# FFN blocks: units of the second product set between the Strassen pairs of the next quarter

## The chip, the cores and the metric

The kernel runs on one core of a Trainium2 chip. The time is the device time of one execution in microseconds (us); of several runs the median is taken.

## The reference

A forward pass over 512 positions of width 1024 in float32: four layers with different mixers, each followed by an FFN, and a fifth block with its own mixers and an FFN. Every FFN is the same computation, and it is the part that this change touches:

```python
def _sqrelu_mlp(h, w1, w2):
    return jnp.square(jax.nn.relu(h @ w1)) @ w2

x = x + _sqrelu_mlp(_rmsnorm(x, norm_mlp_g[i]), mlp_w1[i], mlp_w2[i])
```

Here x is 512 x 1024, w1 is 1024 x 4096 and w2 is 4096 x 1024. The mixers are a gated linear recurrence (twice), a gated spatial unit, a short convolution and, in the last block, a long one with several branches (layer M below), cross attention and an FFN.

## The kernel before

**Stages.** The program emits twelve stages one behind the other: A0 F0 B F1 C F2 A1 F3 M X G N2. F0 to F3 and G are the five FFN blocks, A0, B, C and A1 the mixers between them, M and X the mixers of the last block, N2 the last norm. Activations stand transposed, so a tile of 128 x 512 holds 128 of the 1024 (or 4096) features for all 512 positions.

**Products.** A float32 product is made from three matmuls in fp32r: each operand is split into a high half (a cast) and a low half (what is left), and `mm3` (L896 to L898) adds high x high, high x low and low x high in psum. Weights are split on the chip: ScalarE casts the high half (whi), VectorE subtracts it from the raw tile for the low half (wlo).

**Units.** The usual piece of work is a unit: weights of 8 x 128 x 128 (a raw tile of 128 x 1024 that holds eight 128 x 128 blocks), 24 matmuls of 512 columns, one psum tile. Its cast is L839, its low half L840. Two raw tiles (NRAW) and three pairs of weight tiles (NW) go round; weights are prepared two tiles ahead of the product that is being issued (PREP).

**FFN quarters.** An FFN block (`ffn`, L993) goes through w1's 4096 columns in four quarters. The first product of quarter 0 is eight plain units on the unscaled x with the norm's factor applied behind (relu, square and split make u, eight tiles per quarter, as uhi and ulo). The first product of quarters 1 to 3 is four Strassen pairs each: `pair` (L1058) makes two tiles of u from two column blocks of w1 with seven products of half the positions in place of eight, 84 matmuls of 256 columns. Four of the seven products use sums of weight blocks that `_mixed` (L780) makes on VectorE (ws, L796 and L798), each product's weights (128 x 512) are cast by L825 and subtracted by L807, and two consecutive products share one weight tile. The low half is put off: `_low` (L803) issues it together with the next product's cast. What the products give is combined on VectorE into two tiles: tu, the odd one (cm at L1074 and L1075, tu at L1078), and cy, the even one (L1080 and L1083). Each of the two then goes through three ScalarE instructions (relu L940, square L1005, cast L1006) and one VectorE subtraction (ulo, L1009). These are put off too, in the list `todo`: tu's to the pair's products 5 and 6, cy's to the next pair's products 0 and 1; in a quarter's last pair cy's are issued at once.

Behind a quarter's first product, `project` (L973) runs the eight units of the second product, which add their result to x (L979). A unit needs all eight u of its quarter; the two u that come last are asked for last (`ks`). So the order of work in a block is: eight units of w1, eight units of w2, then three times four pairs and eight units of w2.

**What stands beside.** During quarter 0 a side thread (`background`) normalizes x and prepares the operands for the Strassen products, 32 steps: two at each unit of w1 but the first, one at each third step of the units of w2, the rest behind them.

**Extra products.** The first four products of each run of pairs (EXTRA) are prepared ahead of the three weight tiles, in eight slots (whx, wlx) of the common store for activation tiles, which has 75 slots of 128 x 512 (NSLOT).

**Order.** The pairs and units run in the order of the code. In stages with several threads, such as M, a planner (`schedule`, L413) picks the next step by a model of the engines' clocks; that clock runs on from the program's first stage to the last, and the picks depend on where it stands.

The lines that fix which weights are ready when:

```python
    def _low(self):
        if self.late is not None:
            low, w, high = self.late
            self.nc.vector.tensor_sub(low, w, rt(high))
            self.late = None
...
        while self.pos + len(self.ready) < n and self.tids[self.pos + len(self.ready)] <= self.base[self.pos] + PREP:
            while self.loaded < n and self._load():
                pass
            self._prep()
```

Of the kernel before, what the change touches and what calls it, by code (L numbers as in the profile page):

```python
# [13 lines left out]
ALU = mybir.AluOpType  # L14
# [3 lines left out]
P = 128  # L18
# [12 lines left out]
NRAW = 2  # L31
NW = 3
PREP = 2
EXTRA = 4
NSLOT = 75
LAST = 0
TOL = 300
# [161 lines left out]
def rt(t):  # L199
    return t.bitcast(F32)  # L200
# [451 lines left out]
class Net:  # L652
    def __init__(self, tc, nc, es, d, plan=None):
# [4 lines left out]
        else:  # L658
# [4 lines left out]
            for unit in self.order:  # L663
                two = isinstance(unit[0], str)
                run = run + 1 if two else 0
                extra = two and run <= EXTRA
                t += not (extra or two and half)
# [325 lines left out]
    def ffn(self, inp, nxt, w1, w2):  # L993


        nc = self.nc
        hn, op, todo = [], {}, []

        def relu2(t, k, when):


            def rounded():
                u[k] = self.t("uhi", S, F32R), self.t("ulo", S, F32R)
                self.act(t, t, AF.Relu)
                nc.scalar.square(t, t)  # L1005
                nc.scalar.copy(u[k][0], t)  # L1006

            def rest():
                nc.vector.tensor_sub(u[k][1], t, rt(u[k][0]))  # L1009

            return [(when[0], rounded), (when[1], rest)]

        def square(t):
            hi, lo = self.t("uhi", S, F32R), self.t("ulo", S, F32R)
            nc.scalar.square(t, t)
            nc.scalar.copy(hi, t)
            nc.vector.tensor_sub(lo, t, rt(hi))
            return hi, lo

        def normed():  # L1020
            r = inp.scale()
            for m in range(NCH):
                t = self.t("hn")
                nc.vector.scalar_tensor_tensor(t, inp.xs[m], self.v(inp.gname, inp.g0 + m), r, ALU.mult, ALU.mult)
                hn.append(t)
                yield

        def background():
            yield from normed()
            yield from operands()  # L1030

        def operands():

            a, b = HALF
            for c in range(4):
                p, q = hn[c], hn[c + 4]
                s, t = self.t("ts"), self.t("ts")
                nc.vector.tensor_sub(s[:, a], p[:, b], p[:, a])
                nc.vector.tensor_sub(s[:, b], q[:, b], s[:, a])
                yield  # L1040
                nc.vector.tensor_sub(t[:, a], q[:, b], p[:, b])
                nc.vector.tensor_sub(t[:, b], q[:, a], s[:, b])
                yield
                if c % 2 == 0:
                    raw = self.t("thi", S, F32R), self.t("tlo", S, F32R)
                h = HALF[c % 2]
                nc.scalar.copy(raw[0][:, h], p[:, a])
                nc.vector.tensor_sub(raw[1][:, h], p[:, a], rt(raw[0][:, h]))
                op[0, c] = [x[:, h] for x in raw]
                yield  # L1050
                for src, i, j in ((q, 1, 2), (s, 4, 5), (t, 6, 3)):
                    w = self.t("thi", S, F32R), self.t("tlo", S, F32R)
                    nc.scalar.copy(w[0], src)
                    nc.vector.tensor_sub(w[1], src, rt(w[0]))
                    op[i, c], op[j, c] = [x[:, a] for x in w], [x[:, b] for x in w]
                    yield

        def pair(s0, s1, j, last):  # L1058

            a, b = HALF  # L1060
            ps, add = {}, nc.vector.tensor_add
            for i, (k, bank, h) in enumerate(PRODUCTS):
                w = self.w_pair(s0, s1, i)
                for f in [f for n, f in todo if n == i]:
                    f()
                if h == 0:
                    ps[bank] = self.psum()
                for c in range(4):
                    self.mm3(ps[bank][:, HALF[h]], w[0][:, c], w[1][:, c], *op[k, c], c == 0, c == 3, 357)
                if i == 1:  # L1070
                    y, m = self.t("cy"), self.t("cm")
                    nc.scalar.copy(y[:, a], ps[0][:, a])
                elif i == 2:
                    add(m[:, a], y[:, a], ps[0][:, b])  # L1074
                    add(m[:, b], m[:, a], ps[1][:, a])  # L1075
                elif i == 4:
                    t = self.t("tu")
                    add(t.rearrange("p (c n) -> p c n", c=2), m[:, None, b].to_broadcast([P, 2, 256]),  # L1078
                        ps[2].rearrange("p (c n) -> p c n", c=2))
                    add(y[:, b], m[:, a], ps[2][:, b])  # L1080
                    todo[:] = relu2(t, j + 1, (5, 6))
                elif i == 6:
                    add(y, y, ps[3])  # L1083
                    todo[:] = relu2(y, j, (0, 1))
                    if last:
                        while todo:
                            todo.pop(0)[1]()
                self.lock(i < 6)
                yield

        for q in range(4):
            u = []
            if q == 0:
                side = background()
                for j in range(8):
                    ps = yield from self.mm(w1[j], inp.h)
                    r = inp.scale()
                    t = self.t("tu")
                    nc.vector.scalar_tensor_tensor(t, ps, 0.0, r, ALU.max, ALU.mult)
                    u.append(square(t))  # L1100
                    if j:
                        next(side, None)
                        next(side, None)
                    yield
                product = self.project(w2[q], u, None)
                for n, need in enumerate(product):
                    if n % 3 == 0:
                        next(side, None)
                    yield need
                for _ in side:  # L1110
                    pass
                hn.clear()
                continue
            u = [None] * 8
            for j in range(0, 8, 2):
                yield from pair(w1[q * 8 + j], w1[q * 8 + j + 1], j, j == 6)
            yield from self.project(w2[q], u, nxt if q == 3 else None, ks=(0, 1, 2, 3, 4, 5, 7, 6))


    def lru_consts(self):  # L1120
# [1052 lines left out]
```

## Time and profile before

| | before |
|---|---|
| three runs, us | 3529.70, 3520.67, 3526.14 (median 3526.14) |
| profiled execution, us | 3520.22 |
| its span, us | 3518.4 |
| mean granted clock of TensorE | 0.993 |
| TensorE busy (matmuls), us | 3404.5 |
| TensorE weight loads, us | 2783.7 |
| VectorE busy, us | 2313.7 |
| ScalarE busy, us | 1531.6 |
| GpSimd busy, us | 524.5 |
| DMA | 334.91 MB, 95 GB/s on the mean |

The span goes from the first to the last instruction of the profiled execution; its own time lies 1.8 us above it. In the profile PE is TensorE's matmuls, PEld its weight loads, DVE is VectorE, ACT is ScalarE, POOL is GpSimd, SP issues the loads. L840 is line 840 of the kernel. An instruction is named by what it writes and reads (wlo<-raw,whi), its count by x. A matmul's busy time runs from its start to its modelled end, so that a matmul which is held up in the middle counts as busy for longer.

### The profile page before, as it was taken

To read this page: it belongs to the slowest core of one execution; us is meant where nothing else is said; L and a number is where in the kernel's file an instruction comes from. 1 tells how busy PE (TensorE), PEld (TensorE's weight loads), DVE (VectorE), ACT (ScalarE), POOL (GpSimd) and SP (SyncE) were. 2 spreads that over 40 slices of the span, in tenths; PEclk is the share of its full clock that TensorE was granted. 3 is DMA by queue.
4 is the path that set the end of the run, shared out by engine and by line. 5 is a ranking of instruction groups with operands and counts; after the bars stand their busy time and mean duration, and the time that the engine had idled before them with its cause. 6 is when DMAs were issued, how large, how long until landed. Compare 5 with 4: busy or idle time off the path is not lost. (4 is left out here: it accounts for less than half of the span.)

```text
span 3518.4 us, 48137 instructions
## 1 busy us (share of the span) xinstructions
PE 3404.5 (97%) x18850; PEld 2783.7 (79%) x18850; DVE 2313.7 (66%) x3618; ACT 1531.6 (44%) x2393; POOL 524.5 (15%) x845
## 2 busy tenths in 40 slices
PE   8999999999999999999999999999999999999998
PEld 6778888888887888887877888777767787778887
DVE  7677666567666567666767666776568566567665
ACT  5634444344443234444554444443354344334444
POOL 1020002110001010001011000546245400110002
PEclk9999999999999999999999999999999999999999
DMA  3223222222223323222223222332223344223221
GB/s 118 86 84 114 96 96 84 84 90 90 96 96 103 96 90 102 96 96 85 86 83 119 84 91 87 108 95 84 73 82 125 91 131 154 63 80 115 96 96 61
DMA packets 127237, 334.91 MB, mean 95 GB/s; under 512 B 18592, under 2 KB 21792, under 8 KB 127008
## 3 DMA queue, kind: packets, MB, share of 16 engines
q1 hardware_dynamic: 119712, 322.37, 29.1%
q0 software_dynamic: 7296, 9.46, 1.1%
q8 instruction: 148, 2.42, 0.3%
q14 instruction: 81, 0.66, 0.1%
HBM read 317.07 MB, written 14.68 MB: 94 GB/s over the span
## 5 line engine op out<-in xcount | busy, mean ns | idle before, releaser
L840 DVE TENSOR_TENSOR wlo<-raw,whi 128x1024 fp32r<-128x1024 f32 (+3 forms) x466 | 609.6, 1308 | 178.3 <-ACT whi L839 168.5
L839 ACT CAST whi<-raw 128x1024 fp32r<-128x1024 f32 (+3 forms) x466 | 463.6, 999 | 492.6 <-PE ps L897 370.1
L896 PE MATMUL ps<-hhi,whi 128*128 128x512 f32 x1512 | 619.8, 410 | 11.6 <-ACT whi L839 6.1
L898 PE MATMUL ps<-hhi,wlo 128*128 128x512 f32 x1512 | 600.8, 397 | 7.4 <-DVE wlo L840 7.4
L897 PE MATMUL ps<-hlo,whi 128*128 128x512 f32 x1512 | 601.2, 398 | 5.8 <-DVE hlo L476 5.8
L896 PE MATMUL ps<-uhi,whi 128*128 128x512 f32 (+1 forms) x1296 | 508.6, 392 | 10.4 <-ACT uhi L1006 10.4
L897 PE MATMUL ps<-ulo,whi 128*128 128x512 f32 (+1 forms) x1296 | 508.3, 392 | 3.4 <-DVE ulo L1009 3.4
L898 PE MATMUL ps<-uhi,wlo 128*128 128x512 f32 (+1 forms) x1296 | 507.1, 391 | 0.0
L898 PE MATMUL ps<-thi,wlo 128*128 128x256 f32 x1440 | 415.1, 288 | 24.2 <-DVE wlo L807 20.6
L896 PE MATMUL ps<-thi,whi 128*128 128x256 f32 x1440 | 407.5, 283 | 7.0 <-ACT whi L825 6.7
L897 PE MATMUL ps<-tlo,whi 128*128 128x256 f32 x1440 | 404.1, 281 | 0.0
L896 PEld LDWEIGHTS ps<-hhi,whi 128*128 128x128 f32 x1512 | 286.0, 189 | 86.7 <-ACT hhi L475 6.9
L898 PEld LDWEIGHTS ps<-hhi,wlo 128*128 128x128 f32 x1512 | 285.7, 189 | 76.1 <-DVE wlo L840 9.1
L897 PEld LDWEIGHTS ps<-hlo,whi 128*128 128x128 f32 x1512 | 285.6, 189 | 72.3 <-DVE hlo L476 10.6
L898 PEld LDWEIGHTS ps<-thi,wlo 128*128 128x128 f32 x1440 | 270.9, 188 | 45.7 <-DVE wlo L807 45.7
L896 PEld LDWEIGHTS ps<-uhi,whi 128*128 128x128 f32 x1296 | 243.3, 188 | 71.2 <-ACT uhi L1006 16.8
L897 PEld LDWEIGHTS ps<-ulo,whi 128*128 128x128 f32 x1296 | 243.3, 188 | 62.8 <-DVE ulo L1009 8.1
L898 PEld LDWEIGHTS ps<-uhi,wlo 128*128 128x128 f32 x1296 | 243.3, 188 | 55.3
L896 PEld LDWEIGHTS ps<-thi,whi 128*128 128x128 f32 x1440 | 271.1, 188 | 13.1 <-ACT whi L825 13.1
L979 DVE TENSOR_TENSOR x<-x,ps 128x512 f32<-128x512 f32 x176 | 120.5, 685 | 230.2 <-PE ps L898 230.2
L897 PEld LDWEIGHTS ps<-tlo,whi 128*128 128x128 f32 x1440 | 271.2, 188 | 0.0
L896 PE MATMUL ps<-hi,whi 128*128 128x512 f32 x616 | 247.6, 402 | 9.0 <-ACT hi L945 5.2
(371 smaller groups left out, 5363.5 us busy)
## 6 DMA issues: line engine op xcount, KB each, us to landing
raw<-in_mlp_dram SPq DMA_DIRECT2D x160, 512.0 KB, 3.7
raw<-in_mlp_dram SPq DMA_DIRECT2D x192, 256.0 KB, 5.1
raw<-in_u_ffn_w_dram SPq DMA_DIRECT2D x40, 512.0 KB, 3.7
raw<-in_a_win_dram SPq DMA_DIRECT2D x39, 512.0 KB, 3.6
raw<-in_w_rest_dram SPq DMA_DIRECT2D x34, 512.0 KB, 3.7
raw<-in_w_rkv_dram SPq DMA_DIRECT2D x26, 512.0 KB, 3.7
raw<-in_c_win_dram SPq DMA_DIRECT2D x24, 512.0 KB, 3.7
raw<-in_u_ffn_w_dram SPq DMA_DIRECT2D x48, 256.0 KB, 5.2
```

The lines of the kernel that those rows point to most:

```text
L839: nc.scalar.copy(h[:, c], r[:, c])
L840: nc.vector.tensor_sub(l[:, c], r[:, c], rt(h[:, c]))
L896: nc.tensor.matmul(ps, wh, xh, start=start, stop=False)
L897: nc.tensor.matmul(ps, wh, xl, start=False, stop=False)
L898: nc.tensor.matmul(ps, wl, xh, start=False, stop=stop)
L979: self.nc.vector.tensor_add(self.x[m], self.x[m], ps)
```

## The change

Behind the eight units of quarter 0's first product, the units of a quarter's second product no longer run as eight in a row behind four pairs in a row. A string gives the order for each quarter q of 0 to 2: U is a unit of the second product of quarter q, P a pair of quarter q + 1's first product. For quarter 0 it is UUUUUUPUUPPP, for quarters 1 and 2 UUUUPUUPUUPP. The eight units of quarter 3 come last, as before. Per block five pairs (of twelve) then stand alone between units, four stand in twos and three in a three. The list `todo` is worked off at a pair's products as before, or at every odd step of a unit. The side thread advances at every even step of a unit of quarter 0. EXTRA is 0, so all products of pairs are prepared in the three weight tiles. Two quarters of u (eight tiles each, uhi and ulo) are alive at the same time.

```diff
@@ -31,7 +31,7 @@
 NRAW = 2
 NW = 3
 PREP = 2
-EXTRA = 4
+EXTRA = 0
 NSLOT = 75
 LAST = 0
 TOL = 300
@@ -996,7 +996,7 @@
         nc = self.nc
         hn, op, todo = [], {}, []
 
-        def relu2(t, k, when):
+        def relu2(t, u, k, when):
 
 
             def rounded():
@@ -1055,14 +1055,14 @@
                     op[i, c], op[j, c] = [x[:, a] for x in w], [x[:, b] for x in w]
                     yield
 
-        def pair(s0, s1, j, last):
+        def pair(s0, s1, u, j, last):
 
             a, b = HALF
             ps, add = {}, nc.vector.tensor_add
             for i, (k, bank, h) in enumerate(PRODUCTS):
                 w = self.w_pair(s0, s1, i)
-                for f in [f for n, f in todo if n == i]:
-                    f()
+                while todo and todo[0][0] <= i:
+                    todo.pop(0)[1]()
                 if h == 0:
                     ps[bank] = self.psum()
                 for c in range(4):
@@ -1078,43 +1078,49 @@
                     add(t.rearrange("p (c n) -> p c n", c=2), m[:, None, b].to_broadcast([P, 2, 256]),
                         ps[2].rearrange("p (c n) -> p c n", c=2))
                     add(y[:, b], m[:, a], ps[2][:, b])
-                    todo[:] = relu2(t, j + 1, (5, 6))
+                    todo.extend(relu2(t, u, j + 1, (5, 6)))
                 elif i == 6:
                     add(y, y, ps[3])
-                    todo[:] = relu2(y, j, (0, 1))
+                    todo.extend(relu2(y, u, j, (0, 1)))
                     if last:
                         while todo:
                             todo.pop(0)[1]()
                 self.lock(i < 6)
                 yield
 
-        for q in range(4):
-            u = []
-            if q == 0:
-                side = background()
-                for j in range(8):
-                    ps = yield from self.mm(w1[j], inp.h)
-                    r = inp.scale()
-                    t = self.t("tu")
-                    nc.vector.scalar_tensor_tensor(t, ps, 0.0, r, ALU.max, ALU.mult)
-                    u.append(square(t))
-                    if j:
-                        next(side, None)
-                        next(side, None)
-                    yield
-                product = self.project(w2[q], u, None)
-                for n, need in enumerate(product):
-                    if n % 3 == 0:
+        def unit(q, m):
+            ps = yield from self.mm(w2[q][m], us[q], ks=late if q else None)
+            nc.vector.tensor_add(self.x[m], self.x[m], ps)
+            yield
+
+        us, late = [[None] * 8 for _ in range(4)], (0, 1, 2, 3, 4, 5, 7, 6)
+        side = background()
+        for j in range(8):
+            ps = yield from self.mm(w1[j], inp.h)
+            r = inp.scale()
+            t = self.t("tu")
+            nc.vector.scalar_tensor_tensor(t, ps, 0.0, r, ALU.max, ALU.mult)
+            us[0][j] = square(t)
+            if j:
+                next(side, None)
+                next(side, None)
+            yield
+        for q in range(3):
+            u, j, m = us[q + 1], 0, 0
+            for step in "UUUUUUPUUPPP" if q == 0 else "UUUUPUUPUUPP":
+                if step == "P":
+                    yield from pair(w1[q * 8 + 8 + j], w1[q * 8 + 9 + j], u, j, j == 6)
+                    j += 2
+                    continue
+                for n, need in enumerate(unit(q, m)):
+                    if n % 2 == 1 and todo:
+                        todo.pop(0)[1]()
+                    if q == 0 and n % 2 == 0:
                         next(side, None)
                     yield need
-                for _ in side:
-                    pass
-                hn.clear()
-                continue
-            u = [None] * 8
-            for j in range(0, 8, 2):
-                yield from pair(w1[q * 8 + j], w1[q * 8 + j + 1], j, j == 6)
-            yield from self.project(w2[q], u, nxt if q == 3 else None, ks=(0, 1, 2, 3, 4, 5, 7, 6))
+                m += 1
+            us[q] = None
+        yield from self.project(w2[3], us[3], nxt, ks=late)
 
 
     def lru_consts(self):
```

Every engine executes the same instructions as before (16415 rows on TensorE in both), but for two table loads fewer on ScalarE in layer M; what changes is their order. Three places show it.

VectorE before, from the end of a quarter's third pair (ulo of tu, the last sum of y) into its fourth (mixed weights ws, low halves wlo, ulo of y, the sums cm and tu):

```order
L807 TENSOR_TENSOR wlo<-raw,whi 128x512
L1009 TENSOR_TENSOR ulo<-tu,uhi 128x512
L1083 TENSOR_TENSOR cy<-cy,ps 128x512
L807 TENSOR_TENSOR wlo<-ws,whi 128x512
L798 TENSOR_TENSOR ws<-raw,ws 128x512
L807 TENSOR_TENSOR wlo<-raw,whi 128x512
L1009 TENSOR_TENSOR ulo<-cy,uhi 128x512
L1074 TENSOR_TENSOR cm<-cy,ps 128x256
L1075 TENSOR_TENSOR cm<-cm,ps 128x256
L807 TENSOR_TENSOR wlo<-ws,whi 128x512
L840 TENSOR_TENSOR wlo<-raw,whi 128x1024
L1078 TENSOR_TENSOR tu<-cm,ps 128x512
```

VectorE at the end of a pair that stands alone, changed: the same sums tu and cy and the same ulo, but with the low halves of the two units that follow (L840) among them, and the ws of the next pair behind.

```order
L807 TENSOR_TENSOR wlo<-ws,whi 128x512
L840 TENSOR_TENSOR wlo<-raw,whi 128x1024
L1078 TENSOR_TENSOR tu<-cm,ps 128x512
L1080 TENSOR_TENSOR cy<-cm,ps 128x256
L840 TENSOR_TENSOR wlo<-raw,whi 128x1024
L1009 TENSOR_TENSOR ulo<-tu,uhi 128x512
L1083 TENSOR_TENSOR cy<-cy,ps 128x512
L796 TENSOR_TENSOR ws<-raw 128x512
L798 TENSOR_TENSOR ws<-ws,raw 128x512
L807 TENSOR_TENSOR wlo<-raw,whi 128x512
L798 TENSOR_TENSOR ws<-raw 128x512
L1009 TENSOR_TENSOR ulo<-cy,uhi 128x512
```

So the low half of one unit stands ahead of the sum for tu and that of a second ahead of ulo at the end of a single pair too, where at the third pair's end before only weights of the next pair stood. The next pair's first ws and low half come behind the last sum of y.

ScalarE at a quarter's last pair, before: both casts of the first two units' weights (128 x 1024) stand ahead of tu's three instructions, and y's three follow.

```order
L1072 COPY cy<-ps 128x256
L839 CAST whi<-raw 128x1024 x2
L940 ACTIVATE tu<-tu 128x512
L1005 ACTIVATE tu<-tu 128x512
L1006 CAST uhi<-tu 128x512
L940 ACTIVATE cy<-cy 128x512
L1005 ACTIVATE cy<-cy 128x512
L1006 CAST uhi<-cy 128x512
L839 CAST whi<-raw 128x1024 x6
```

ScalarE at the end of a three of pairs, changed (quarter 0's string ends with PPP, and the next pair's last product of 128 x 512 stands alone in its weight tile):

```order
L1072 COPY cy<-ps 128x256
L825 CAST whi<-ws 128x512
L839 CAST whi<-raw 128x1024
L940 ACTIVATE tu<-tu 128x512
L1005 ACTIVATE tu<-tu 128x512
L1006 CAST uhi<-tu 128x512
L839 CAST whi<-raw 128x1024
L940 ACTIVATE cy<-cy 128x512
L1005 ACTIVATE cy<-cy 128x512
L1006 CAST uhi<-cy 128x512
L839 CAST whi<-raw 128x1024 x2
```

The second unit's cast has moved behind tu's three instructions; y's three stay behind both.

ScalarE at the end of layer M, before: sigmoids (ld), casts of weights, and among them the rsqrt of a norm (ysq, r, ysq) between two table loads, ahead of the casts (hi) that the last product there needs.

```order
L940 ACTIVATE ld<-ld 128x512 x4
L839 CAST whi<-raw 128x1024
L939 ACT_TABLE_LOAD
L940 ACTIVATE ysq<-ms 128x512
L940 ACTIVATE r_25952<-ysq 128x512
L958 ACTIVATE ysq<-r_25952 128x512
L939 ACT_TABLE_LOAD
L940 ACTIVATE ld<-ld 128x512 x4
L839 CAST whi<-raw 128x1024
L940 ACTIVATE ld<-ld 128x512
L839 CAST whi<-raw 128x1024
L945 CAST hi<-y 128x512
```

The same place, changed: no line of M is edited, the planner's picks differ.

```order
L940 ACTIVATE r_25856<-ysq 128x512
L958 ACTIVATE ysq<-r_25856 128x512
L945 CAST hi<-y 128x512 x7
L1442 COPY vt<-ps 128x512 x2
L939 ACT_TABLE_LOAD
L940 ACTIVATE ld<-ld 128x512 x4
L839 CAST whi<-raw 128x1024
L940 ACTIVATE ld<-ld 128x512 x4
L839 CAST whi<-raw 128x1024
L940 ACTIVATE ld<-ld 128x512
L839 CAST whi<-raw 128x1024
L945 CAST hi<-y 128x512
```

The rsqrt and seven of the casts (hi<-y) now stand ahead of the sigmoids, with one table load in place of two behind it.

## Rows read from the trace of the kernel before

**Rows 1.** The page: span, and the engines' busy time, share, instructions.

```profile
span 3518.4 us, 48137 instructions
...
PE 3404.5 (97%) x18850; PEld 2783.7 (79%) x18850; DVE 2313.7 (66%) x3618; ACT 1531.6 (44%) x2393; POOL 524.5 (15%) x845
```

**Rows 2.** Windows in one quarter: stretch, length, busy time and instructions, granted clock, DMA.

```profile
417.94:427.86 9.92, 9.92 (x86) 9.91 (x84) 4.96 (x9) 3.45 (x7) 0.00 (x0) 1.00 0.44 166
427.86:437.80 9.94, 9.94 (x87) 9.94 (x85) 7.87 (x14) 5.43 (x11) 0.00 (x0) 1.00 0.00 0
437.80:448.76 10.96, 10.46 (x86) 10.05 (x85) 9.63 (x18) 7.79 (x14) 0.00 (x0) 1.00 0.01 2
448.76:462.15 13.39, 11.81 (x86) 10.37 (x85) 10.35 (x18) 8.63 (x14) 0.00 (x0) 1.00 0.00 0
462.15:469.15 7.00, 6.09 (x26) 4.43 (x25) 4.18 (x7) 4.75 (x8) 0.00 (x0) 1.00 0.53 153
469.15:474.71 5.56, 5.56 (x26) 4.50 (x25) 2.60 (x3) 1.05 (x2) 0.00 (x0) 1.00 0.49 156
```

**Rows 3.** The same over all four pairs, first and last of fifteen quarters.

```profile
327.82:371.99 44.17, 42.07 (x337) 40.23 (x336) 32.80 (x57) 25.33 (x44) 0.00 (x0) 1.00 0.12 40
...
3413.22:3457.41 44.19, 42.16 (x337) 40.32 (x336) 32.80 (x57) 25.30 (x44) 0.00 (x0) 1.00 0.10 37
```

**Rows 4.** The same, the last of fifteen first units behind pairs.

```profile
3457.41:3464.43 7.02, 6.12 (x27) 4.44 (x25) 4.21 (x7) 4.71 (x7) 0.00 (x0) 1.00 0.51 149
```

**Rows 5.** Waits of PE, whole span: total us, times, longest.

```profile
PE ps L898 <- DVE wlo L807: 20.6, 75, 0.4
...
PE ps L896 <- ACT uhi L1006: 10.4, 15, 0.7
...
PE ps L896 <- ACT whi L825: 6.7, 15, 0.5
...
PE ps L897 <- DVE ulo L1009: 3.4, 15, 0.2
```

**Rows 6.** Timeline of DVE at a quarter's end: start, length, instruction, [idle before].

```profile
460.71 1.22 DVE L840 TENSOR_TENSOR wlo<-raw,whi 128x1024 fp32r<-128x1024 f32 x1
461.84 0.68 DVE L1078 TENSOR_TENSOR tu<-cm,ps 128x512 f32<-128x512 f32 x1
462.44 0.41 DVE L1080 TENSOR_TENSOR cy<-cm,ps 128x256 f32<-128x256 f32 x1
462.77 1.22 DVE L840 TENSOR_TENSOR wlo<-raw,whi 128x1024 fp32r<-128x1024 f32 x1
464.54 0.69 DVE L1009 TENSOR_TENSOR ulo<-tu,uhi 128x512 fp32r<-128x512 f32 x1 [0.55 <-ACT uhi L1006]
465.15 0.68 DVE L1083 TENSOR_TENSOR cy<-cy,ps 128x512 f32<-128x512 f32 x1
```

**Rows 7.** Timeline of ACT at the same end.

```profile
458.70 1.99 ACT L839 CAST whi<-raw 128x1024 fp32r<-128x1024 f32 x2
...
467.19 0.62 ACT L1006 CAST uhi<-cy 128x512 fp32r<-128x512 f32 x1
```

**Rows 8.** Timeline of PE at the end of layer M, and a window there.

```profile
2920.81 0.39 PE L898 MATMUL ps<-hi,wlo 128*128 128x512 f32 x1
2926.41 0.79 PE L896 MATMUL ps<-hi,whi 128*128 128x512 f32 x1 [5.21 <-ACT hi L945]
...
2932.37 0.39 PE L898 MATMUL ps<-hi,wlo 128*128 128x512 f32 x1
...
2926.40:2931.80 5.40, 4.50 (x10) 3.22 (x11) 3.37 (x5) 1.00 (x2) 0.00 (x0) 0.50 0.55 194
```

**Rows 9.** Groups of ACT instructions, 2899 to 2927 us: busy, mean ns, idle before.

```profile
L940 ACT ACTIVATE ld<-ld 128x512 f32<-128x512 f32 x9 | 5.0, 621 | 0.0
L945 ACT CAST hi<-y 128x512 fp32r<-128x512 f32 x8 | 4.4, 627 | 3.8 <-DVE y L1782 3.8
...
L939 ACT ACT_TABLE_LOAD x3 | 3.8, 1283 | 0.1
```

## The prediction

> **What bounds the kernel now.** I read the page first: TensorE is busy for 3404.5 of 3518.4 us, VectorE for 2313.7 and ScalarE for 1531.6 [rows 1]. So TensorE is the bound, and 114 us of idle time seem to be all that there is to win. But busy time counts a matmul that is stretched by a wait as busy, so next I read the windows, cut at the first matmul of each pair in one quarter [rows 2]. Four equal pairs of 84 matmuls take 9.92, 9.94, 10.96 and 13.39 us: the first two run at 0.118 us per matmul, the third loses 1.04 and the fourth 3.47. The first product unit behind them takes 7.00 us where the next takes 5.56 (24 matmuls at 0.232): 1.44 lost. The windows over whole quarters show that this is the same everywhere: fifteen stretches of four pairs (five blocks, three quarters each), the first 44.17 and the last 44.19 us [rows 3], against 4 x 9.92 = 39.7, and fifteen first units of about 7.02 [rows 4]. That is 15 x (4.5 + 1.45) = **89 us** of TensorE's time in this pattern.
>
> The list of waits gives only 20.6 + 6.7 + 10.4 + 3.4 = 41 us to the same four waits [rows 5]: for the low half of a pair's weights, for the high half, and for the two halves of the last u. I take the 89, since start-to-start distances hold whatever is counted busy. The Trainium skill (Perfetto Trace Analysis, Identifying the Most-Contended Engine) says the same of the matmul busy share, that it is no good measure because matmuls are pipelined. By the 41 alone, the block's part of the sum below would be 41/89 of it, 24 us in place of 51.
>
> Why do pairs wait? VectorE works in its queue's order, and two 128x512 instructions behind each other start 0.60 apart [rows 6]. A pair needs fifteen of these (seven low halves, four mixed weights, the sum for tu, the last sum for y, two ulo) and three of half the width at 0.33: 15 x 0.60 + 3 x 0.33 = 10.0 us, against 9.92 on TensorE. There is no slack, so each moment in which VectorE waits for ScalarE, and ScalarE for VectorE's sum, comes off the lead. The lead is what stands ready at the quarter's start. Of a product unit VectorE needs one 1024-wide low half (1.13, from 460.71 to the next start at 461.84) and one x sum, 1.73 of 5.56 us. So four pairs in a row use the lead up, and eight units in a row leave VectorE idle.
>
> **The change part by part.** (1) *The pairs.* No matmul, no product and no byte is added or removed. Of twelve pairs per block, five now stand alone between units, four stand in twos and three in a three. Between two single pairs stand two units, so a period needs 10.0 + 2 x 1.73 = 13.5 us of VectorE for 9.92 + 11.1 = 21 of TensorE: the four products that two weight tiles hold are ready again at each new pair. Single pairs: no wait, so 0. A two begins with four products ready, not with eight as a quarter does now, but weight tiles pair its products as now (0 and 1, 2 and 3, and so on), so from its seventh product on each cast is issued at the same step as in the first two pairs of rows 2, which lose nothing: 0, up to 1.04 if the shorter lead shows. A three's third pair is the third pair of rows 2: 1.04 lost, up to 3.47 if it behaves like a fourth. Per block the pairs lose 1.04 in place of 3 x 4.5 = 13.5.
>
> (2) *The ends.* Units of a quarter need every u of it, so three times per block a run of pairs is still followed by units that need its last u. Now the chain is: low half of the second unit's weights (462.77), ulo of tu only at 464.54, sum for y at 465.15, three ScalarE instructions to 467.8, while TensorE asks for that u 18 + 3 matmuls (4.87 us) after 462.15 [rows 6, 7]. After a two, ScalarE and VectorE have the same order as now (both casts of 1.0 us ahead of tu's ReLU): 1.45 each. After a three, 21 products leave the last alone in its weight tile; the second unit's cast (1.04) now stands behind tu's three ScalarE instructions, and VectorE's 1.13 behind that cast and ahead of y's sum: 2.2 later, 1.45 + 2.2 = 3.7. Per block 3.7 + 2 x 1.45 = 6.6 in place of 4.35. A unit behind a single pair belongs to the quarter before and has every u.
>
> (3) *The slots.* Without the four extra products, their casts go to the weight tiles; same number, same width: 0. They take eight of the 75 act slots out of use, and two quarters of u put sixteen in; the tiles that stand at once stay at most 70 of 75, so no tile waits for a fresh release. The operands that VectorE prepares beside the first quarter's units move from every third step to every second: four in a unit, about 4 x 0.6 = 2.4 us beside 1.73 of 5.56: 0. SP's loads alternate kinds in the order of use; they wait for the same two raw tiles, and a unit's raw is asked for a whole pair or two units ahead: 0.
>
> Sum over five blocks: 5 x (13.5 + 4.35 - 1.04 - 6.6) = **51 us** saved. Bounds: 28 us (each two loses 1.04, the three's last pair 3.47, ends as above) and 89 (no wait is left).
>
> (4) *Mixing layer M.* The planner's clock runs on through all phases, so the other order of the blocks before it shifts its picks in M, though no line of M is edited. What moves is the tail: now TensorE waits 5.21 us for the last y's high half, and behind that wait it runs at a granted 0.50, which is 1.2 GHz, to 2931.8 [rows 8]. From 2920.81 to 2932.37 stand twelve matmul starts; twelve at 0.232 are 2.8 us, so 8.8 are lost. The y is late because its rsqrt stands behind four sigmoids, between two table loads of 1.28 [rows 9], and its last sums behind seven products with psum. In the change the rsqrt is ahead of the sigmoids (both table loads gone) and the sums behind two such products. From the rsqrt to that high half ScalarE then has seven casts (8 take 4.4 us) and two copies like them, one table load, nine sigmoids (5.0) and three casts of weights at 1.0 [rows 7, 9], some 14 us; TensorE has 23 groups of three matmuls at 0.232, 16 us, ahead of that need. I take 8 of 8.8. Ends: a gain of 9, and, since the other picks may open a wait like this one elsewhere, a loss of 9.
>
> Sum: 51 + 8 = 59. The profiled execution took 3520.2 (span 3518.4 and 1.8 around it), so 3461; it lies 5.9 under the median of the runs, 3526.1. Against that median: **3467 us**.
>
> **The rivals.** *A, all of it goes*: VectorE's slack between pairs lets sums run ahead, no pair waits and the ends come in time. For it: VectorE is behind at every end now. Against: the ends' order is the same. 3526 - 89 - 9 = 3428.
>
> *B, the lead is what counts*: the four products ahead held the waits off to the sixteenth product; with four fewer ready they begin four earlier. Then the second pair of a two loses 1.04, a three 1.04 + 3.47, ends as above: 2 x 1.04 + 4.5 + 6.6 = 13.2 per block in place of 17.85, so 23 saved, and 8: 3495. For it: the regular wait at the same product in all fifteen stretches. Against: pair two of rows 2 loses nothing with those four long used up. The Trainium skill (Perfetto Trace Analysis, Optimization Strategy) has this as a rule: a gap that repeats can mean too few buffers for the next tile; by it, taking slots away is wrong. The trace does not settle it.
>
> *C, slower*: a unit's cast and subtraction stand ahead of each pair's sums at all twelve pair ends of a block, now at three. If those were paid by TensorE with two low halves each (2 x 1.22 = 2.4), the 60 ends would cost 146 against 98 won: 3574. It decides from 98/60 = 1.6 us per end. For it: the chain of rows 6. Against: behind a single pair nothing near needs that pair's u.
>
> *D, the waits only move*: the next unit waits for weights in place of the pair, because its cast now comes late in a pair. Then 3526, or 3518 with M. Against: the cast is issued at the pair's fifth product, 4.25 us ahead.
>
> **How the numbers follow.** Forecast 0.58, A 0.13, B 0.15, C 0.07, D 0.07. Under 0.3% (10.6 us) a measurement of this kernel can't tell from no change. Faster by more: forecast, A and B, 0.86; within: D, 0.07; slower: C, 0.07. The range goes from A's 3428 over the bounds of the forecast's terms to B's 3495 and a little beyond: 3428 to 3500; C, D and the lower half of A are left out.
>
> **What would show it.** Windows by pair: single pairs at 9.9, both pairs of a two at 9.9 to 10.2, a three's last at about 11; first units behind a two at 7.0, behind the three at about 9.2, all others at 5.56. Waits for a pair's low half fall from 75 to some ten. M's tail shows no wait of 5 us. It is wrong if single pairs take over 10.5 us, if units behind them take over 6, or if M's gap stays.

## The result, and the profile after

The changed kernel takes 3481.45 us (median of four runs, 3475.65 to 3489.07), the kernel before 3524.19 (four runs): a ratio of 0.9879, 95% interval 0.9853 to 0.9904, faster by 34 to 52 us. The forecast was 3467, range 3428 to 3500: right in sign and range, too hopeful by 14 us. From here on the two profiled executions are compared, 3520.22 and 3475.65 us: 44.6 less, where 59 was the sum.

The page after, the rows that answer to [rows 1]:

```profile
span 3473.8 us, 48153 instructions
...
PE 3377.3 (97%) x18850; PEld 2778.3 (80%) x18850; DVE 2308.4 (66%) x3618; ACT 1529.3 (44%) x2391; POOL 521.4 (15%) x845
```

TensorE's busy time fell by 27 us with the same 18850 matmuls, and its share stayed at 97%: 27 of the 44.6 us that went had been counted as busy. Windows over the five FFN blocks, each from its first unit of w2 to its last matmul (the eight units of w1 ahead lie outside), give the place. The last line of each answer, before and after, holds the total:

```profile
sum 1578.55, PE 1532.26 PEld 1327.04 DVE 1036.30 ACT 705.91 POOL 96.66; mean PE 306.45 PEld 265.41 DVE 207.26 ACT 141.18 POOL 19.33
```

```profile
sum 1543.83, PE 1512.57 PEld 1325.03 DVE 1033.65 ACT 706.19 POOL 96.62; mean PE 302.51 PEld 265.01 DVE 206.73 ACT 141.24 POOL 19.32
```

So 34.7 of the 44.6 us came out of the FFN blocks (51 forecast) and 9.9 from elsewhere (8 forecast, in M). What happens inside a block is shown by windows of the change in the first FFN block, cut as in [rows 2]: a unit behind a single pair, the three pairs of the three, the two units behind them, then the second pair of a two and the unit behind it.

```profile
326.23:331.75 5.52, 5.52 (x26) 4.50 (x25) 3.74 (x6) 2.20 (x4) 0.00 (x0) 1.00 0.69 212
337.31:347.23 9.92, 9.92 (x85) 9.91 (x84) 8.91 (x16) 4.40 (x8) 0.00 (x0) 1.00 0.01 2
347.23:357.62 10.39, 10.20 (x86) 10.00 (x85) 7.32 (x14) 6.02 (x11) 0.00 (x0) 1.00 0.01 2
357.62:369.37 11.75, 10.69 (x86) 10.07 (x85) 10.45 (x18) 8.21 (x14) 0.00 (x0) 1.00 0.00 0
369.37:378.43 9.06, 6.40 (x27) 4.35 (x25) 4.15 (x7) 5.70 (x9) 0.00 (x0) 1.00 0.55 177
378.43:385.57 7.14, 7.14 (x26) 5.67 (x24) 2.59 (x3) 1.04 (x2) 0.00 (x0) 0.76 0.84 248
448.89:459.28 10.39, 10.20 (x86) 10.00 (x85) 7.35 (x13) 7.40 (x12) 0.00 (x0) 1.00 0.00 1
459.28:466.30 7.02, 6.12 (x27) 4.43 (x25) 4.20 (x7) 4.72 (x7) 0.00 (x0) 1.00 0.72 232
```

All five blocks show the same: 25 single pairs at 9.91 to 9.96, fifteen second pairs at 10.33 to 10.39, five third pairs at 11.75 to 11.81, five first units behind the three at 9.03 to 9.45, ten behind a two at 7.02 to 7.06, and units behind single pairs at 5.52 to 5.60. The list of TensorE's waits, over the whole span (answers to [rows 5]):

```profile
PE ps L896 <- ACT uhi L1006: 16.1, 15, 1.8
...
PE ps L898 <- DVE wlo L807: 7.1, 25, 0.5
PE ps L897 <- DVE ulo L1009: 6.1, 19, 0.6
```

The waits for a pair's low half fell from 75 to 25 (some ten forecast), the wait for its high half is gone, and the waits for the last u (uhi and ulo) grew from 13.8 to 22.2 us: the ends got dearer, as forecast.

### The profile page after: what moved, and what is told of

The parts are those of the page before. It is cut to its first block, busy times and chain, and to the rows that moved or that the text cites. A ratio compares the mean times of both kernels' runs of the same rounds, so it can differ in the third digit from the quotient of the medians.

```text
span 3473.8 us, 48153 instructions
## 1 busy us (share of the span) xinstructions
PE 3377.3 (97%) x18850; PEld 2778.3 (80%) x18850; DVE 2308.4 (66%) x3618; ACT 1529.3 (44%) x2391; POOL 521.4 (15%) x845
## 5 line engine op out<-in xcount | busy, mean ns | idle before, releaser
L840 DVE TENSOR_TENSOR wlo<-raw,whi 128x1024 fp32r<-128x1024 f32 (+3 forms) x466 | 608.9, 1307 | 279.3 <-ACT whi L839 270.3
L898 PE MATMUL ps<-thi,wlo 128*128 128x256 f32 x1680 | 475.1, 283 | 7.8 <-DVE wlo L807 7.1
L897 PE MATMUL ps<-tlo,whi 128*128 128x256 f32 x1680 | 471.8, 281 | 0.0
L896 PE MATMUL ps<-thi,whi 128*128 128x256 f32 x1680 | 471.1, 280 | 0.0
L898 PEld LDWEIGHTS ps<-thi,wlo 128*128 128x128 f32 x1680 | 316.3, 188 | 13.9 <-DVE wlo L807 13.9
L896 PEld LDWEIGHTS ps<-thi,whi 128*128 128x128 f32 x1680 | 316.8, 189 | 1.8
L897 PEld LDWEIGHTS ps<-tlo,whi 128*128 128x128 f32 x1680 | 316.1, 188 | 1.8
L825 ACT CAST whi<-ws 128x512 fp32r<-128x512 f32 x240 | 149.0, 621 | 323.0 <-DVE ws L798 169.6
L897 PE MATMUL ps<-lo,whi 128*128 128x512 f32 x616 | 245.5, 398 | 7.1 <-DVE lo L1258 4.5
```

The costliest lines, as they stand in the source:

```text
L825: nc.scalar.copy(h, w)
L840: nc.vector.tensor_sub(l[:, c], r[:, c], rt(h[:, c]))
L896: nc.tensor.matmul(ps, wh, xh, start=start, stop=False)
L897: nc.tensor.matmul(ps, wh, xl, start=False, stop=False)
L898: nc.tensor.matmul(ps, wl, xh, start=False, stop=stop)
```

## The experiments

Outside the FFN blocks the two programs' orders differ in layers A1 and M alone (6 of A1's 333 steps, 146 of M's 1539). In all runs of the table behind the change these two orders are written out, so that an edit of the FFN blocks cannot move them: at those of the change, but for old_noextra and new_oldpicks, which have those of before. Ratios are to the kernel before on the same chip, with 95% intervals; the fourth column is the total over the five FFN blocks in the profiled execution. Where the blocks are not edited (old_newpicks, new_oldpicks) it repeats that of the kernel before to 0.2 us and that of the change to 1.0.

| run | median us | ratio | FFN blocks us |
|---|---|---|---|
| before | 3524.19 | 1 | 1578.6 |
| the change | 3481.45 | 0.9879 [0.9853, 0.9904] | 1543.8 |
| old_newpicks | 3514.99 | 0.9989 [0.9977, 1.0002] | 1578.4 |
| new_oldpicks | 3482.57 | 0.9892 [0.9876, 0.9909] | 1544.8 |
| old_noextra | 3538.84 | 1.0058 [1.0043, 1.0073] | 1596.8 |
| new_extra2 | 3462.40 | 0.9839 [0.9823, 0.9856] | 1526.5 |
| new_extra4 | 3458.03 | 0.9830 [0.9814, 0.9846] | 1524.1 |
| tu_behind_cast | 3464.09 | 0.9836 [0.9818, 0.9854] | 1527.8 |
| singles | 3460.64 | 0.9825 [0.9805, 0.9845] | 1518.6 |
| unit_behind | 3450.35 | 0.9797 [0.9776, 0.9817] | 1507.4 |
| best | 3430.87 | 0.9741 [0.9726, 0.9755] | 1494.6 |
| best2 | 3434.75 | 0.9757 [0.9740, 0.9774] | 1497.1 |
| best3 | 3430.49 | 0.9740 [0.9727, 0.9754] | 1493.5 |

### The slots: old_noextra, new_extra2, new_extra4

```diff
-EXTRA = 4
+EXTRA = 0
```

> The kernel before with EXTRA at 0 and nothing else (the planner's orders of A1 and M held at those of before). Theory that the lead counts: a run of four pairs then behaves as the change's three does in its first pairs, that is 9.92, 10.39 and 11.77 us, and a fourth pair that loses at least as much as now (13.4 or more): 45.5 us or more per quarter in place of 44.2, 20 us or more over fifteen quarters, 3540 us. Rival (my prediction's step 3: the slots cost nothing, the waits come from VectorE's and ScalarE's order at each pair's end alone): 44.2 per quarter and 3520.

The four pairs of a quarter, with the old order and no extra slots (windows, first quarter of pairs):

```profile
327.34:337.25 9.91, 9.91 (x85) 9.91 (x84) 8.93 (x16) 4.43 (x8) 0.00 (x0) 1.00 0.38 143
337.25:347.62 10.37, 10.17 (x86) 9.97 (x85) 7.29 (x14) 6.02 (x11) 0.00 (x0) 1.00 0.01 3
347.62:359.43 11.81, 10.77 (x86) 10.15 (x85) 10.48 (x19) 8.41 (x15) 0.00 (x0) 1.00 0.01 1
359.43:372.76 13.33, 11.82 (x86) 10.41 (x85) 10.29 (x18) 8.64 (x14) 0.00 (x0) 1.00 0.00 0
```

The lead counts. Second and third pairs are those of the change to a few hundredths, and the fourth is no later than in [rows 2]: 45.4 us per quarter, 18 us lost over the blocks, and a ratio clear of 1. The other way round, the change with extra products:

```diff
-EXTRA = 0
+EXTRA = 2   (new_extra2)
+EXTRA = 4   (new_extra4)
```

> The change with two products of each run of pairs prepared ahead in four act slots (EXTRA 2), orders of A1 and M held. At most 73 of the 75 slots then hold something in an FFN block. Theory that the lead counts: the waits of a run start two products later, so the second pair of a two takes 9.92 in place of 10.39 and the three's last about 11.3 in place of 11.77: 1.4 + 0.5 less per block, some 9 us in all, 3466. Rival (the wait at the end of a second pair is that pair's own chain of sums): 10.39 stays, 3475.

> The change with EXTRA at 4 as in the kernel before, orders of A1 and M held: the other order alone. Lead theory without a lack of slots: second pairs 9.92, the three's last 10.96 as the third pair before, some 11 us less than the change, 3464. Rival: the eight slots beside two quarters of u are too many for 75, so raw tiles and mixed weights wait for a u to be read, and pairs or units that take 9.9 and 5.56 in the change take longer; then at or above 3475.

Second and third pair of the three in new_extra2:

```profile
347.66:357.59 9.93, 9.93 (x87) 9.93 (x85) 7.86 (x14) 5.43 (x11) 0.00 (x0) 1.00 0.01 2
357.59:368.56 10.97, 10.45 (x86) 10.04 (x85) 9.68 (x17) 7.59 (x13) 0.00 (x0) 1.00 0.00 0
```

The first unit behind the three, and a first unit behind a two, in new_extra4:

```profile
367.38:376.39 9.01, 6.38 (x27) 4.36 (x25) 4.11 (x7) 5.70 (x9) 0.00 (x0) 1.00 0.60 171
457.66:463.87 6.21, 5.98 (x25) 4.42 (x24) 3.94 (x5) 4.40 (x6) 0.00 (x0) 1.00 0.83 269
```

Two products ahead already give 9.93 for second pairs and 10.97 for the third, against 10.39 and 11.75, and bring the unit behind a two from 7.02 to 6.2. Four give no more: 9.93, 10.99 and 6.21. In its FFN blocks new_extra4 saves 1578.6 - 1524.1 = 54 us over before, near the 51 of the forecast: its pairs lose what the forecast had for them, its ends behind a two cost 0.8 less each (8 us in all), and a slow unit behind the three, on which the last section tells more, takes 5 us back in three blocks. The second half of the change, no extra slots, gives 20 of the 54 back, some 11 in the pairs and 8 at the ends of twos. The rival of new_extra4, a lack of slots with eight more in use, shows nowhere: single pairs and the units behind them take 9.9 and 5.6 as in the change.

### The ends: tu_behind_cast, singles, unit_behind

```diff
-                    todo.extend(relu2(t, u, j + 1, (5, 6)))
+                    todo.extend(relu2(t, u, j + 1, (6, 6) if last else (5, 6)))
```

> The change with tu's put-off steps in a quarter's last pair moved from products 5 and 6 to product 6: on ScalarE the second unit's cast now stands ahead of tu's three instructions behind the three too, as it does behind a two; nothing else moves there. Theory of step 2: the first unit behind the three falls from 9.05 to about 7.0, and the slow unit behind it (7.1 in three blocks of five) is gone with the long wait: some 3 us per block, 15 in all, 3461. Rival: the end of the three is set by VectorE's lag, so 9.05 stays and the time with it, 3475.

ScalarE and then VectorE at the end of the three in the change (timelines): the second unit's cast stands behind tu's three instructions, and y's first waits 2.49 us for the sum that VectorE makes only after that cast's low half.

```profile
369.75 0.63 ACT L940 ACTIVATE tu<-tu 128x512 f32<-128x512 f32 x1 [2.82 <-DVE tu L1078]
...
371.60 1.05 ACT L839 CAST whi<-raw 128x1024 fp32r<-128x1024 f32 x1
375.14 0.63 ACT L940 ACTIVATE cy<-cy 128x512 f32<-128x512 f32 x1 [2.49 <-DVE cy L1083]
```

```profile
369.03 0.68 DVE L1078 TENSOR_TENSOR tu<-cm,ps 128x512 f32<-128x512 f32 x1
...
372.68 1.23 DVE L840 TENSOR_TENSOR wlo<-raw,whi 128x1024 fp32r<-128x1024 f32 x1 [2.64 <-ACT whi L839]
...
374.43 0.68 DVE L1083 TENSOR_TENSOR cy<-cy,ps 128x512 f32<-128x512 f32 x1
```

In tu_behind_cast, the third pair of the three and the two units behind it (windows):

```profile
357.20:368.95 11.75, 10.68 (x86) 10.07 (x85) 10.46 (x18) 9.27 (x15) 0.00 (x0) 1.00 0.00 0
368.95:375.91 6.96, 6.13 (x26) 4.43 (x25) 4.15 (x7) 4.71 (x7) 0.00 (x0) 1.00 0.72 231
375.91:381.50 5.59, 5.59 (x25) 4.51 (x24) 2.59 (x3) 1.08 (x2) 0.00 (x0) 1.00 0.79 251
```

One cast moved ahead of three instructions takes 2.1 us off each first unit and the slow unit behind it away: 16 us, as expected.

```diff
-            for step in "UUUUUUPUUPPP" if q == 0 else "UUUUPUUPUUPP":
+            for step in "UUUUUPUPUPUP" if q == 0 else "UUPUUPUUPUUP":
```

> The change with strings in which every pair stands alone: UUUUUPUPUPUP for quarter 0, UUPUUPUUPUUP for the others (orders of A1 and M held, no extra slots). All pairs then take 9.92. What is open is the end of a quarter, where a single pair is followed by the units that need its u. Theory of the prediction's step 2 (the odd number of products puts the second unit's cast behind the three instructions on tu): a run of one ends like the run of three, with a first unit of about 9.05 at all three ends of a block, and a dip of the clock behind some: 10.5 to 14 us lost per block against 11.7 in the change, so 3470 to 3487. Rival (the three's end is late because VectorE and ScalarE have fallen behind by its third pair): first units of 6.2 to 7.0, 2 to 4.4 us per block, 3428 to 3440.

A last pair and the first unit behind it (windows), and VectorE's sum for tu in that pair (timeline):

```profile
356.61:366.57 9.96, 9.96 (x86) 9.96 (x84) 7.21 (x12) 4.46 (x8) 0.00 (x0) 1.00 0.07 24
366.57:374.04 7.47, 6.09 (x27) 4.43 (x25) 3.72 (x5) 4.04 (x7) 0.00 (x0) 1.00 0.56 175
```

```profile
364.63 0.68 DVE L1078 TENSOR_TENSOR tu<-cm,ps 128x512 f32<-128x512 f32 x1
```

Neither theory holds alone: the first unit takes 7.5 at all fifteen ends, and all sixty pairs take 9.9. The cast does stand behind tu's three here too, but the sum for tu starts 366.57 - 364.63 = 1.94 us ahead of the pair's end. In the change's three it starts at 369.03, 0.34 ahead of its end. That difference, 1.60, is the difference of the first units, 9.06 - 7.47 = 1.59: an end costs the wrong order of the cast, and on top of it VectorE's lag. Ends with the right order agree: behind a two the sum for tu starts 0.28 to 0.30 ahead of the pair's end in the change and 1.10 to 1.13 ahead in new_extra4, and the first units take 7.02 and 6.21, again 0.8 for 0.8. No run has the right order behind a single pair that ends a quarter.

```diff
-            for step in "UUUUUUPUUPPP" if q == 0 else "UUUUPUUPUUPP":
+            for step in "UUUUUUPUPPPU" if q == 0 else "UUUUPUUPUPPU":
```

> The change with one unit of the old quarter kept behind the last pair: UUUUUUPUPPPU and UUUUPUUPUPPU (orders of A1 and M held, no extra slots). The runs of one, two and three pairs stay. Theory: the waits at the ends are the chain of the last u alone, and 5.56 us of a unit that does not need it cover it: all units at 5.56, the clock does not dip, 6.4 + 1 us less per block, 37 in all, 3439; pairs as in the change (10.39, 11.77). Rival: the wait moves to the weights of the unit behind the pair, whose cast stands among the sums; then first units of 6.5 or more remain, and 3455 or above.

The second and third pair of the three, the old unit behind it and the first that needs the new u (windows):

```profile
341.41:351.93 10.52, 10.19 (x87) 9.99 (x86) 7.39 (x14) 6.14 (x12) 0.00 (x0) 1.00 0.00 0
351.93:363.73 11.80, 10.74 (x87) 10.13 (x85) 10.52 (x18) 8.21 (x14) 0.00 (x0) 1.00 0.01 1
363.73:369.28 5.55, 5.55 (x27) 4.51 (x25) 2.92 (x5) 2.83 (x4) 0.00 (x0) 1.00 0.40 100
369.28:374.80 5.52, 5.52 (x25) 4.50 (x24) 3.25 (x5) 3.79 (x5) 0.00 (x0) 1.00 0.37 106
```

One unit that needs nothing of the last pair covers its whole end: all first units take 5.5 to 5.6, 36 us less in the blocks than the change, while the second pairs pay 0.16 more. As a whole the run missed what was expected, 3450 for 3439: in the profiled execution some 7 us come back in the stretches between the blocks, which this edit does not touch (2.4 in that of A1, 3.9 in that of M and X).

### The planner: old_newpicks, new_oldpicks

```diff
-            i = best[1]
+            i = int(PICKED[len(order)][len(picks)], 16) if len(order) in PICKED else best[1]
```

> The kernel before, with the step orders that the planner chose in the changed kernel for layers A1 and M written out as constants; the FFN blocks are those of before. Theory: of the 44.6 us between the two profiled executions, 34.7 lie inside the five FFN blocks and 9.9 outside, and the 9.9 are the planner's other orders alone. Then layer A1 takes 259.4 us in place of 262.7, M and X together 960.2 in place of 965.7, the FFN blocks stay at 315 us, and the execution takes about 3511. Rival: the tail of M gets shorter because the FFN blocks leave other weights or other slots behind; then A1 and M stay at 262.7 and 965.7, and the time at 3520.

> The change with the step orders of layers A1 and M of the kernel before written out. Theory: the planner's part is real in layer M alone: the wait of 5.2 us for the last y's high half is back, M and X together take 965 to 966 us in place of 960, and layer A1, which stood at 260.5 to 261.8 in four runs with either order, does not answer to it; the execution is some 5 us above the change, 3480. Rival: M's 5 us were chance, as 975.2 with the old order and no extra slots suggests; then 960 to 962 with the old order.

Windows of layer M between the same two of its matmuls, of which the tail is the end: before, new_oldpicks, the change, old_newpicks.

```profile
2680.06:2943.47 263.41, 254.27 (x1926) 200.13 (x1926) 174.90 (x390) 113.03 (x200) 60.49 (x150) 0.99 0.38 117
```

```profile
2654.72:2917.81 263.09, 254.03 (x1927) 200.09 (x1926) 174.79 (x390) 113.03 (x200) 61.26 (x150) 0.99 0.37 117
```

```profile
2647.95:2905.41 257.46, 251.25 (x1926) 198.68 (x1926) 174.56 (x390) 110.60 (x198) 60.24 (x150) 1.00 0.39 119
```

```profile
2676.06:2934.66 258.60, 252.90 (x1926) 199.92 (x1926) 174.29 (x390) 110.69 (x198) 60.96 (x150) 0.99 0.38 119
```

M's part follows the picks and not the FFN blocks. It takes 263.1 to 263.8 in the three profiles with the old picks and 257.1 to 259.9 in the ten with the new, some 5 us. As a whole program old_newpicks cannot be told from no change, since other stretches vary as much. The stretch of layer A1, up to the end of F3's units of w1, took 262.7 before and 259.4 in the change, but 260.5 in old_newpicks and 260.9 in new_oldpicks, so its 3 us answer to neither (1.8 of them are F3's first two units of w1, with a granted clock of 0.96 around them before and 1.00 in the change). Nor does a stretch of M ahead of these windows: it took 145 to 147 us in eleven profiles and 153 in old_noextra and in best3, one with each order, at a granted clock of 0.93.

### A version that beats both: best, best2, best3

```diff
             if j:
                 next(side, None)
                 next(side, None)
+                next(side, None)
...
-            for step in "UUUUUUPUUPPP" if q == 0 else "UUUUPUUPUUPP":
+            for step in "UUUUPUPUPUPU":
```

> One string for all three quarters, UUUUPUPUPUPU: every pair alone, and a unit of the old quarter behind the last one. So that the operands are ready two units earlier, three side steps in place of two at each unit of w1. No extra slots; at most 70 of 75 in use. Theory: one unit between pairs gives VectorE 15.5 us for 11.7 us of work, so no pair waits (9.92), and no end waits (5.56): of the 11.7 us lost per block in the change nearly all go, 3418 to 3425. Rival A: one unit is too little to make up the lead, and from the second pair on each takes 10.39: 7 us per quarter of a block less won, about 3440. Rival B: the third side step makes the units of w1 late on VectorE (above 5.6 each): 8 units by five blocks, each 0.3 late is 12 us.

The first unit behind w1's, a pair, and the old and the new unit behind the last pair (windows):

```profile
282.09:288.87 6.78, 6.11 (x25) 4.43 (x24) 5.35 (x10) 4.43 (x9) 0.00 (x0) 1.00 0.44 137
...
336.46:346.35 9.89, 9.89 (x86) 9.89 (x84) 8.08 (x14) 4.41 (x8) 0.00 (x0) 1.00 0.09 20
361.81:367.39 5.58, 5.58 (x26) 4.52 (x25) 2.43 (x3) 2.99 (x6) 0.00 (x0) 1.00 0.43 146
367.39:372.94 5.55, 5.55 (x25) 4.50 (x24) 3.65 (x4) 2.46 (x3) 0.00 (x0) 1.00 0.34 100
```

No pair and no end waits any more, without an extra slot: 0.9741, and 84 us less in the FFN blocks than before. The median lies 6 us above what was expected. What is left is the first unit behind w1's, 6.6 to 7.1 us in four blocks of five. It is not rival B as it stood: w1's own units, from the third on, take 5.56 as in the change.

```diff
+            for _ in range((0, 3, 3, 3, 3, 3, 3, 1)[j]):   (best2)
+            for _ in range((0, 3, 3, 3, 3, 3, 1, 3)[j]):   (best3)
```

> The kernel of the run best (one string UUUUPUPUPUPU, every pair alone, a unit behind the last) with the side steps at w1's units spread as 3, 3, 3, 3, 3, 3, 1 from the second unit to the last. In best the first unit behind w1's took 6.6 to 7.1 us in four blocks of five, all others 5.56. Theory: the third side step at the last unit of w1 stood ahead of the last u on VectorE; with one there, this unit takes 5.6: 5 us less in all, 3426. Rival: the first unit is late because w1's last u and the norm's factor come late anyway (5.56 in the change, where two stood there, speaks against it): 3431.

> The kernel of best2 with the side steps spread as 3, 3, 3, 3, 3, 1, 3: one step behind w1's seventh unit, three behind the last. Taking steps away behind the last unit left the first unit behind w1's at 6.7 to 7.7 us, and on VectorE it is the steps behind the seventh unit and the low half behind them that stand between the last unit's end and its tu. Theory: with one step there tu starts earlier, ScalarE's square and cast with it, and the first unit takes 5.6 to 5.8; some 5 to 6 us less in all, 3425. Rival: tu is then held by the low half of 1.2 us alone, the steps do not matter, and 6.7 stays; 3430.

As wholes both missed their theory's time, 3426 and 3425, and lie at or above the rival's, 3431 and 3430. In best2 that unit took 6.7 to 7.7: the steps behind the last unit are not the ones in the way. VectorE in best, around the end of w1's last unit at 282.09, has the steps and the low half behind the unit before it ahead of the last tu:

```profile
283.79 0.69 DVE L1054 TENSOR_TENSOR tlo<-hn,thi 128x512 fp32r<-128x512 f32 x1
284.39 1.22 DVE L840 TENSOR_TENSOR wlo<-raw,whi 128x1024 fp32r<-128x1024 f32 x1
285.52 0.69 DVE L1102 SCALAR_TENSOR_TENSOR tu<-ps,r 128x512 f32<-128x512 f32 x1
```

With two of those steps taken out (best3) the unit took 5.7 to 5.9 in three blocks but 6.8 and 7.1 in two. In all three versions the unit's time follows that tu: where it starts 1.9 us behind the end of w1's last unit, the unit takes 5.59, at 2.3 to 2.6 it takes 5.7 to 5.9, and at 3.2 to 4.3 it takes 6.6 to 7.7. In the two blocks of best3 VectorE was already about 1 us further behind at the tu of the unit before; why it was is open. The ratios of the three versions overlap.

## Why the prediction was right, and where its sum failed

- **The mechanism held.** Four pairs in a row eat the lead, units give it back. Single pairs lose nothing, at 25 places. The 89 us of [rows 3] and [rows 4] were the right measure: best took 84 out of the blocks and new_extra4 54, more than the 41 that the list of waits [rows 5] holds in all. (By the 41 the blocks' sum would have been 24, which is nearer to the measured 34.7 than 51 is. That would have been luck: it starts from too small a loss and lacks the same two terms as the 51.) The Trainium skill (Perfetto Trace Analysis, Optimization Strategy) says that where the most-contended engine changes over time, interleaving those regimes may help. The pairs, with VectorE at its limit, and the units, with TensorE at it, are such regimes, and best agrees by 84 us.
- **The step that failed is part (3), "The slots: 0"** (with part (1), which gave second pairs no loss because the first two of [rows 2] lose nothing). Those two stood on the four products ahead. Without them each second pair loses some 0.46 and the third 1.85 in place of 1.04: 15 x 0.46 + 5 x 0.8 = 11 us of pairs that the sum did not have. The bounds did (up to 1.04 and 3.47), but the signs named for this did not come: second pairs lie above 9.9 to 10.2, the third above about 11. The rows could not show it, as all fifteen quarters had the extra products. Rival B had the mechanism, waits that begin earlier, with a chance of 0.15, but priced them as a shift by four products: 1.04 for the second pair of a two and 4.5 for a three, where 0.46 and 2.3 were measured. The time, 3481, came out half way between the forecast's 3467 and B's 3495. The Trainium skill (Perfetto Trace Analysis, Optimization Strategy) has the rule that was set beside B, that a gap that repeats can mean too few buffers. It bears out where pairs stand in a row: four products more ahead take 20 us off the change, four fewer add 18 to the old order. Where each pair stands alone (singles, best) no pair waits without them.
- **The ends** were right: 3.5 behind the three (3.7 forecast) and 1.46 behind a two (1.45), with the cause shown by tu_behind_cast. The 1.45 was taken over from ends where VectorE's sum for tu starts 0.3 us ahead of the pair's end, and it held because the twos have the same 0.3; with four products ahead (new_extra4) it is 0.65. Not in the sum was the unit behind the three's first: 7.0 to 7.1 us in three blocks, 6.37 in one, 5.57 in one, 5.3 us in all, at a lowered clock (0.76 in the first block).
- **Layer M** was right in kind, 5.2 in place of 8. That all of the 9.9 us outside the blocks lie so near the 8 is luck: the rest of them came from stretches that answer to neither order. The tail, 48.29 us before, takes 43.13. The wait for the high half [rows 8] is gone and the clock stays at 1.00 there, but two others came, of 1.54 us (for a sum of ld) and 2.48 us (for the last y's low half). I followed ScalarE's queue and TensorE's, and not VectorE's: the last y's high half is there at 2888.4, and its low half starts only at 2891.15, behind six sums of ld and two low halves of weights; the last of these and the low half are these rows (timeline of VectorE in the change):

```profile
2890.01 1.22 DVE L840 TENSOR_TENSOR wlo<-raw,whi 128x1024 fp32r<-128x1024 f32 x1
2891.15 0.68 DVE L946 TENSOR_TENSOR lo<-y,hi 128x512 fp32r<-128x512 f32 x1
```

- **The other rivals.** A did not come, since ends and second pairs kept their waits. C had its order of instructions but not its price: at the 25 ends of single pairs the units' casts stand among the sums, and these cost nothing. D did not come: units behind single pairs take 5.56.

Inside the blocks forecast and measurement then meet: 51 - 11 - 5.3 and 1 back at the ends is 35.7, against 34.7.

## What to carry to other kernels

When two kinds of work with different limits follow each other, interleave them, and end a run with a piece that needs nothing of it: here one such piece behind the last pair was worth more (36 us) than putting the order at the end right (16). Products prepared ahead still count where two or three pieces of the expensive kind stand together; where each stands alone, they can go. Price a removed buffer from a place that had none; if the trace has no such place, put the middle of its bounds into the sum and not nothing. Here that is 0.52 for a second pair and 2.26 for the third, where 0.46 and 1.85 were measured.

## What the runs showed that was not expected

The clock. Behind the three's end TensorE stood still for 1.84 us (timeline of TensorE in the change):

```profile
377.13 0.49 PE L896 MATMUL ps<-uhi,whi 128*128 128x512 f32 x1 [1.84 <-ACT uhi L1006]
```

It started this one matmul, waited 0.23 more, and in the next unit the granted clock fell: 0.76 on the mean of that unit, between its two levels of 2.4 and 1.2 GHz, which costs 1.6 us. In the second FFN block the same waits, of 1.83 and 0.22 us, were followed by no fall in the next unit:

```profile
879.04:884.60 5.56, 5.56 (x25) 4.50 (x24) 2.58 (x3) 1.04 (x2) 0.00 (x0) 1.00 0.85 241
```

Over the change, new_oldpicks, new_extra2 and new_extra4 the second unit behind the three was slow 16 times in 20; behind the ends of 6.2 to 7.5 us in the same four runs, singles and tu_behind_cast, never. So a wait of 2 us can cost almost twice its length, or no more than its length, and what decides which was not tried.
